# RWKV-7 recurrence on one core: centring, key transposes and variance on parts of the array, the solve written beside the inner product, and state updates and inverse steps pinned in program order

## The chip, the core and the metric

The kernel runs on one core of one Trainium2 chip. The metric is the device time of one execution in microseconds (us). Nothing is shared with other cores. Engines are called as in the profile: PE is the matmul engine (PEld its weight loads), DVE the vector engine, ACT the scalar engine, POOL the general engine, SP the engine that issues most DMAs.

## What is computed

Sixteen learned tokens and 256 tokens, 272 in all, with 2048 features go through two layers, each a token mixer and a squared-ReLU MLP. Layer 0 mixes by RWKV-7, layer 1 by gated linear attention (GLA). The change lies wholly in layer 0's recurrence, whose 32 heads of 64 features each carry a 64x64 state, and in what stands right behind it: a group norm for each head, a bonus, a gate and the output projection. Cut to that:

```python
def step(S, inp):
    r_t, w_t, k_t, v_t, a_t, b_t = inp
    sa = jnp.einsum('bhvk,bhk->bhv', S, a_t)
    S = S * w_t[:, :, None, :] + sa[..., None] * b_t[:, :, None, :] + v_t[..., None] * k_t[:, :, None, :]
    y = jnp.einsum('bhvk,bhk->bhv', S, r_t)
    return S, y
...
_, y = lax.scan(step, S0, xs)
...
mu = jnp.mean(y, axis=-1, keepdims=True)
var = jnp.mean(jnp.square(y - mu), axis=-1, keepdims=True)
y = ((y - mu) * lax.rsqrt(var + RW_GN_EPS)).reshape(B, T, D) * ln_w + ln_b
bonus = (jnp.sum(rh * kh * r_k, axis=-1, keepdims=True) * vh).reshape(B, T, D)
out = ((y + bonus).astype(x.dtype) * g) @ w_o
```

## The kernel before, in words

**Chunks and groups.** The scan is done in chunks of 64 tokens: four full ones and a last one of 16 tokens (`c` = 0 to 4). The 2048 features lie as 16 tiles of 128 partitions by 272 tokens (`hres` holds v and later y; `rr` the bonus), two heads to a tile. The recurrence runs for two groups of 16 heads (`g` = 0 and 1, 8 tiles each), one after the other. Within a chunk the tokens depend on each other through a triangular matrix for each head, which is inverted; then the chunk is a row of small products.

**A chunk's products on PE**, in fp32, each function a batch of 64x64 products over the 16 heads: `centre` (L671) takes the values of a chunk, token-major and with the head's mean removed, into `uv`; `keys` (L684) transposes the keys into `bkt`; `inner` (L694) applies the scores within the chunk to the values; `state` (L720, L722) applies the carried state `S`, on quadrants of the array in an order written out by hand; `solve` (L731) applies the inverse; `carry` (L740) and `learn` (L746) sum the new state in a PSUM bank, from which DVE writes `S` with the decay (`tt(sb, pS, ...)` on L747, shown as L300, the helper's line); `emit` (L755) makes y. ACT copies results from PSUM (uv on L677 and L734, bkt on L686, the scaled copy `rs` on L702).

**The inverses.** `invert` (L542) runs 30 elimination steps of two DVE operations each on `sysA` (shown as `upd<-sysA` and `sysA<-sysA,upd`, L300) for a batch of blocks of 32 tokens, four batches in all (two chunks or three of each group); the result goes out by DMA and comes back into the score tiles `AM` (`AM<-invd`, L565), and `merge` (L648, L658) joins blocks of 32 to blocks of 64. `scores` (L525) makes the masked scores of the next batches (masks on DVE, L528).

**Norm.** `norm(g)` covers four feature tiles of a group at a time: squares on ACT, the sum over a head on PE (`self.bones`, L773), the gate's product (L776), a logarithm and an exponential on ACT, and the products and sums on DVE (L781, L300, L784).

**Weights beside it.** The v projection and the output projection run in the same stretch, spread between the phases: `R(n)` issues n steps of three fp32r products (`mm3`, L163 to L165: hi x hi, hi x lo, lo x hi). Their weights come by DMA in pieces of 128x1024 (`raw`, three buffers) and are split into `hi` by ACT (L140) and `lo` by DVE (L141), two halves each. One piece lasts eight steps, and the SP queue holds weight loads and the loads of the inverses in one order.

**Order.** Within `manual_schedule(engines={PE})` the PE instructions stand in program order; DVE, ACT and SP instructions are put in order by a scheduler. What stands where on PE is set by numbers: `GAPS` gives the R steps of each chunk ahead of the solve and ahead of `learn`, `MARK` the count of R steps at which each `merge` begins, and `some(inv, n)` how many inverse steps are written at a place. PSUM tags and buffers: `pj` 2, `pm` 1, `pt` 2, `pry` 1, `pu` 2.

Of the kernel before, what the change touches and what calls it, by code (L numbers as in the profile page):

```python
# [46 lines left out]
GAPS = [(4, 2), (4, 2), (4, 2), (4, 3), (5, 5)]  # L47

MARK = [120, 170, 244, 302]
# [5 lines left out]
class Kern:  # L55
# [242 lines left out]
    def rwkv(self, done):  # L298
# [243 lines left out]
        def invert(b):  # L542
# [9 lines left out]
            for s in range(1, 31):  # L552
                k, m = 31 - s, s
                w = self.t(lp, [P, 256], "upd", 1)[:n, : k * m].rearrange("p (a b) -> p a b", a=m)
                tt(w, X[:n, s : s + 1, s + 1 :].to_broadcast([n, m, k]), X[:n, :m, s : s + 1].to_broadcast([n, m, k]))
                tt(X[:n, :m, s + 1 :], X[:n, :m, s + 1 :], w, ALU.add)
                yield
# [107 lines left out]

        def centre(g, c):
            full, n, nr = geom(c)[:3]
            pv = self.pm()
            for p in range(4):
                for e in range(2):  # L670
                    nc.tensor.matmul(pv[64 * e : 64 * e + nr, p * P : (p + 1) * P], hres[:, 8 * g + 4 * e + p, c * C : c * C + nr],  # L671
                                     self.cent, start=True, stop=True)
            x = uvs[g, c] = self.t(kp, [P, 16, 64], "uv", 2)
            if not full:
                nc.gpsimd.memset(x[0 : 2 * n], 0.0)
            for e in range(2):
                nc.scalar.copy(x[:nr, 8 * e : 8 * e + 8], pv[64 * e : 64 * e + nr].rearrange("p (h v) -> p h v", h=8))  # L677

        def keys(g, c):
            bkts[g, c] = self.t(kp, [P, 8, P], "bkt", 1)  # L680
            for e in range(2):
                pb = self.pm() if e else self.ptr()
                for p in range(4):
                    nc.tensor.transpose(pb[:, p * P : (p + 1) * P], BKs[c > 1][:, 4 * e + p, c % 2 * 128 : c % 2 * 128 + 128],  # L684
                                        self.ident)
                nc.scalar.copy(bkts[g, c][:, 4 * e : 4 * e + 4], pb.rearrange("p (h v) -> p h v", h=4))  # L686


        def inner(g, c):
# [3 lines left out]
            for h in range(16):  # L693
                nc.tensor.matmul(ra[at[h % 2], h // 2], am[:n, h, :n], uv[:n, h], start=h < 2, stop=c == 0 and h > 13)  # L694
            if c == 0:
# [29 lines left out]
        def solve(g, c):  # L725
            full, n, nr, am, lo, up, at = geom(c)
            uv, rs, pu = uvs[g, c], ras[g, c, "rs"], bank(self.pu())
            nu = n if full else 16
            for h in range(16):
# [592 lines left out]
```

## Time and profile before

| what | value |
|---|---|
| median of three runs | 2402.7 us (2400.86 to 2403.1) |
| the profiled execution | 2402.54 us |
| its span | 2400.8 us |
| granted PE clock, mean | 0.997 |
| PE busy | 2360.9 us |
| DVE busy | 1611.9 us |
| ACT busy | 1242.4 us |

Engine rows give busy time, share of the span and the number of instructions. A timeline row gives start, duration, engine, line, operation, output and inputs, tile and shape, and in brackets the idle time before it and what ended it. The records of matmuls overlap, so the cost of a matmul is read as the distance from one start to the next. In a fp32 product an instruction leaves two records.

### The profile page before, as it was taken

The page shows a single profiled execution, that of the slowest core. Times are in us where ns is not written, and L with a number is a line of the kernel's source. Part 1 is how long each engine was busy: PE and PEld are TensorE (multiplying, and loading weights), DVE is VectorE, ACT ScalarE, POOL GpSimd, SP SyncE. Part 2 cuts the span into 40 slices and gives each one's busy share as a digit, 9 for nine tenths or more (in the row PEclk, how much of TensorE's full clock was granted, in tenths as well). Part 3 has the DMA queues.
Part 4 walks back from the last instruction along what each step waited for, and adds up shares of the span by engine and source line. Part 5 has one row for each costly group of instructions (what it writes and reads, how often), then busy time and mean ns, then how long its engine had stood idle before and what let it go on. Part 6 is the DMA issues. An engine that isn't in the chain of part 4 may idle for free. (4 is left out here: it accounts for less than half of the span.)

```text
span 2400.8 us, 48047 instructions
## 1 busy us (share of the span) xinstructions
PE 2360.9 (98%) x19689; PEld 2244.1 (93%) x19689; DVE 1611.9 (67%) x2734; ACT 1242.4 (52%) x1975; POOL 6.6 (0%) x20
## 2 busy tenths in 40 slices
PE   9999999899999999999999999999999999999998
PEld 8888888889999999999999999999999999999997
DVE  8777886858655555555556777767666666666666
ACT  6376644556555445445345556555555445445444
POOL 0000000000000000000000000000000000000000
PEclk9999999999999999999999999999999999999999
DMA  6578864524555555555555554455555555555554
GB/s 210 169 235 293 248 190 146 146 83 163 183 187 193 187 191 191 188 193 186 192 189 190 196 181 167 159 176 193 182 201 200 200 201 200 202 202 202 201 201 169
DMA packets 160732, 455.34 MB, mean 190 GB/s; under 512 B 34112, under 2 KB 50624, under 8 KB 160512
## 3 DMA queue, kind: packets, MB, share of 16 engines
q1 hardware_dynamic: 160512, 452.27, 55.8%
q8 instruction: 154, 2.52, 0.4%
q14 instruction: 66, 0.54, 0.1%
HBM read 433.86 MB, written 18.35 MB: 188 GB/s over the span
## 5 line engine op out<-in xcount | busy, mean ns | idle before, releaser
L141 DVE TENSOR_TENSOR lo<-raw,hi 128x1024 fp32r<-128x1024 f32 (+1 forms) x818 | 927.4, 1140 | 534.1 <-ACT hi L140 525.9
L140 ACT CAST hi<-raw 128x1024 fp32r<-128x1024 f32 (+1 forms) x818 | 794.6, 979 | 939.4 <-PE pj L164 546.8
L163 PE MATMUL pj<-x,hi 128*128 128x272 f32 (+1 forms) x2624 | 748.6, 285 | 1.7 <-DVE hres L300 1.0
L165 PE MATMUL pj<-x,lo 128*128 128x272 f32 (+1 forms) x2624 | 734.5, 280 | 4.3 <-DVE lo L141 4.1
L164 PE MATMUL pj<-x,hi 128*128 128x272 f32 (+1 forms) x2624 | 734.0, 280 | 0.2 <-DVE x L240 0.2
L163 PEld LDWEIGHTS pj<-x,hi 128*128 128x128 f32 x2624 | 498.1, 190 | 10.2 <-issue 3.7
L165 PEld LDWEIGHTS pj<-x,lo 128*128 128x128 f32 x2624 | 498.2, 190 | 7.2 <-DVE lo L141 6.5
L164 PEld LDWEIGHTS pj<-x,hi 128*128 128x128 f32 x2624 | 498.2, 190 | 3.6 <-issue 1.4
L196 PE MATMUL pj<-x,hi 128*128 128x512 f32 x1280 | 419.9, 382 | 0.1
L197 PE MATMUL pj<-x,lo 128*128 128x256 f32 x1280 | 348.8, 273 | 0.0
L196 PE MATMUL pj<-h,hi 128*128 128x512 f32 x1008 | 330.3, 382 | 0.0
L163 PE MATMUL pj<-h,hi 128*128 128x272 f32 (+1 forms) x1040 | 290.1, 279 | 0.0
L164 PE MATMUL pj<-h,hi 128*128 128x272 f32 (+1 forms) x1040 | 290.1, 279 | 0.0
L165 PE MATMUL pj<-h,lo 128*128 128x272 f32 (+1 forms) x1040 | 290.1, 279 | 0.0
L197 PE MATMUL pj<-h,lo 128*128 128x256 f32 x1008 | 274.8, 273 | 0.0
L196 PEld LDWEIGHTS pj<-x,hi 128*128 128x128 f32 x1280 | 241.9, 189 | 34.1 <-DVE x L996 0.4
L197 PEld LDWEIGHTS pj<-x,lo 128*128 128x128 f32 x1280 | 245.7, 192 | 0.3 <-DVE lo L141 0.2
L196 PEld LDWEIGHTS pj<-h,hi 128*128 128x128 f32 x1008 | 190.5, 189 | 26.5
L163 PEld LDWEIGHTS pj<-h,hi 128*128 128x128 f32 x1040 | 196.6, 189 | 0.0
L164 PEld LDWEIGHTS pj<-h,hi 128*128 128x128 f32 x1040 | 196.6, 189 | 0.0
L165 PEld LDWEIGHTS pj<-h,lo 128*128 128x128 f32 x1040 | 196.6, 189 | 0.0
L197 PEld LDWEIGHTS pj<-h,lo 128*128 128x128 f32 x1008 | 193.5, 192 | 0.0
(270 smaller groups left out, 2077.2 us busy)
## 6 DMA issues: line engine op xcount, KB each, us to landing
raw<-mlp_w_d SPq DMA_DIRECT2D x512, 512.0 KB, 3.3
raw<-gla_in_d SPq DMA_DIRECT2D x98, 512.0 KB, 3.2
raw<-w_rkv_d SPq DMA_DIRECT2D x80, 512.0 KB, 3.9
raw<-gla_o_d SPq DMA_DIRECT2D x32, 512.0 KB, 4.3
raw<-w_r_d SPq DMA_DIRECT2D x16, 512.0 KB, 3.3
raw<-rw_oQ_d SPq DMA_DIRECT2D x16, 512.0 KB, 3.2
ard<-ar SPq DMA_DIRECT2D x16, 288.0 KB, 3.4
bkd<-bk SPq DMA_DIRECT2D x16, 288.0 KB, 3.5
```

The costliest lines, as they stand in the source:

```text
L140: nc.scalar.copy(hi[:, h], raw[:, h])
L141: nc.vector.tensor_tensor(out=lo[:, h], in0=raw[:, h], in1=hi[:, h].bitcast(F32), op=ALU.subtract)
L163: nc.tensor.matmul(out, hi[:, ws], xh, start=first, stop=False)
L164: nc.tensor.matmul(out, hi[:, ws], xl, start=False, stop=False)
L165: nc.tensor.matmul(out, lo[:, ws], xh, start=False, stop=last)
L196: nc.tensor.matmul(wide, hi[:, ws], xt, start=kt == 0, stop=False)
L197: nc.tensor.matmul(one, lo[:, ws], xt[:, 0], start=False, stop=kt == nk - 1)
```

## The change

Centring (`centre`) is done for two chunks at once, in four quadrants of 64x64 each, into two PSUM banks (`pm` and `pt`); `uv` gets three buffers, and centring is called for chunks 0 and 1, 2 and 3, and 4. `keys` makes 16 half-row transposes on 64 partitions each, in two banks. `solve(c)` and `inner(c + 1)` are issued alternately, head by head, for the first three chunks. In `norm`, the variance of two feature tiles is made together in four quadrants, two banks; the squares of all four tiles are made first (`ysq` four buffers), the gate weights are loaded two tiles ahead, and the logarithm of the second tile is done in two halves. The state update and the inverse steps of the batches behind the first are kept in program order on DVE. `GAPS`, `MARK` and the counts of inverse steps are new, and `scores(2, ...)` all lie in the merge of chunk 2.

On DVE, in group 0, the update of `S` behind chunk 0 stood behind step 10 of the inverse (`128x10x21`). Before:

```order
L300 TENSOR_TENSOR upd_4394<-sysA_1980 128x210
L300 TENSOR_TENSOR sysA_1980<-sysA_1980,upd_4394 128x10x21
L300 TENSOR_TENSOR S_3508<-pu_4428,WC_105 128x512
L300 TENSOR_TENSOR upd_4443<-sysA_1980 128x220
L300 TENSOR_TENSOR sysA_1980<-sysA_1980,upd_4443 128x11x20
```

And now, at the same place in the program:

```order
L300 TENSOR_TENSOR upd_4507<-sysA_1980 128x240
L300 TENSOR_TENSOR sysA_1980<-sysA_1980,upd_4507 128x16x15
L300 TENSOR_TENSOR upd_4510<-sysA_1980 128x238
L300 TENSOR_TENSOR sysA_1980<-sysA_1980,upd_4510 128x17x14
L300 TENSOR_TENSOR S_3508<-pu_4513,WC_105 128x512
L300 TENSOR_TENSOR upd_4571<-sysA_1980 128x234
```

The update has moved behind step 17 (`128x17x14`); which step it stands behind is now what the program writes.

On DVE in group 1, where `norm(1)` (rows `ysq`, `r` and `hres`) and the inverse run beside each other. Before, with step 5 of the inverse written around the first tile of the norm and step 6 behind it:

```order
L300 TENSOR_TENSOR sysA_1980<-sysA_1980,upd_6121 128x4x27
L300 TENSOR_TENSOR upd_6124<-sysA_1980 128x130
L781 SCALAR_TENSOR_TENSOR ysq_5885<-hres_72,vecs_126,ysq_5885 128x272
L300 TENSOR_TENSOR sysA_1980<-sysA_1980,upd_6124 128x5x26
L300 TENSOR_TENSOR r_19_93<-r_19_93,ysq_5885 128x272
L300 TENSOR_TENSOR upd_6163<-sysA_1980 128x150
L784 SCALAR_TENSOR_TENSOR hres_72<-r_19_93,vecs_126,pt_5997 128x272
```

Now (the lines of the norm are 810 and 813 in the new file; `ysq_5972` is the third tile of the norm):

```order
L300 TENSOR_TENSOR hres_72<-pj_6122,hres_72 128x272
L810 SCALAR_TENSOR_TENSOR ysq_5972<-hres_72,vecs_126,ysq_5972 128x272
L141 TENSOR_TENSOR lo_6275<-raw_6272,hi_6274 128x512 x2
L300 TENSOR_TENSOR r_21_95<-r_21_95,ysq_5972 128x272
L300 TENSOR_TENSOR upd_6256<-sysA_1980 128x84
L813 SCALAR_TENSOR_TENSOR hres_72<-r_21_95,vecs_126,pt_6230 128x272
L300 TENSOR_TENSOR sysA_1980<-sysA_1980,upd_6256 128x3x28
L810 SCALAR_TENSOR_TENSOR ysq_5974<-hres_72,vecs_126,ysq_5974 128x272
L300 TENSOR_TENSOR upd_6259<-sysA_1980 128x108
```

Step 3 (`128x3x28`) and all that follow have moved behind the third tile of the norm, and the update of `S` behind chunk 0 of group 1 stands behind step 16 there, where it stood behind step 14 before.

On PE, in group 0, the first solve (L731) was followed by the centring of chunk 1 (L671), and its inner product (L694) came behind `learn` (L746). Before:

```order
L731 MATMUL pu_4397<-rs_4352,AM_402_1979 64x64 x16
L671 MATMUL pm_4416<-cst_125,hres_72 64x128 x8
...
L746 MATMUL pu_4428<-uv_4298,bkt_4308 64x64 x16
L694 MATMUL pu_4484<-uv_4425,AM_402_1979 64x64 x16
L755 MATMUL pry_4501<-AM_402_1979,uv_4298 64x64 x16
```

Now solve (L742) and inner product (L702) alternate, and weight products follow:

```order
L742 MATMUL pu_4445<-rs_4415,AM_402_1979 64x64
L702 MATMUL pu_4447<-uv_4375,AM_402_1979 64x64
...
L742 MATMUL pu_4445<-rs_4415,AM_402_1979 64x64
L702 MATMUL pu_4447<-uv_4375,AM_402_1979 64x64
L163 MATMUL pj_4328<-x_1904,hi_4380 128x272
L164 MATMUL pj_4328<-x_1904,hi_4380 128x272
```

The inner product has moved ahead of `learn` and into the solve. The diff:

```diff
@@ -44,9 +44,9 @@
-GAPS = [(4, 2), (4, 2), (4, 2), (4, 3), (5, 5)]
-
-MARK = [120, 170, 244, 302]
+GAPS = [(2, 4), (5, 3), (5, 4), (4, 5), (5, 5)]
+
+MARK = [120, 180, 244, 308]
@@ -552,8 +552,9 @@
             for s in range(1, 31):
...
                 w = self.t(lp, [P, 256], "upd", 1)[:n, : k * m].rearrange("p (a b) -> p a b", a=m)
-                tt(w, X[:n, s : s + 1, s + 1 :].to_broadcast([n, m, k]), X[:n, :m, s : s + 1].to_broadcast([n, m, k]))
-                tt(X[:n, :m, s + 1 :], X[:n, :m, s + 1 :], w, ALU.add)
+                keep = tc.keep_in_program_order if b else lambda x: x
+                keep(tt(w, X[:n, s : s + 1, s + 1 :].to_broadcast([n, m, k]), X[:n, :m, s : s + 1].to_broadcast([n, m, k])))
+                keep(tt(X[:n, :m, s + 1 :], X[:n, :m, s + 1 :], w, ALU.add))
                 yield
             for rows in some_rows:
@@ -663,27 +664,34 @@
...
+        half = lambda q: slice(HEAD * q, HEAD * q + HEAD)
+        heads = lambda x: x.rearrange("p (h v) -> p h v", h=8)
+
         def centre(g, c):
             full, n, nr = geom(c)[:3]
-            pv = self.pm()
-            for p in range(4):
-                for e in range(2):
-                    nc.tensor.matmul(pv[64 * e : 64 * e + nr, p * P : (p + 1) * P], hres[:, 8 * g + 4 * e + p, c * C : c * C + nr],
-                                     self.cent, start=True, stop=True)
-            x = uvs[g, c] = self.t(kp, [P, 16, 64], "uv", 2)
-            if not full:
-                nc.gpsimd.memset(x[0 : 2 * n], 0.0)
-            for e in range(2):
-                nc.scalar.copy(x[:nr, 8 * e : 8 * e + 8], pv[64 * e : 64 * e + nr].rearrange("p (h v) -> p h v", h=8))
+            pvs = [self.pm(), self.ptr()]
+            for p in range(8):
+                for i in range(1 + full):
+                    for q in range(2):
+                        o = (c + i) * C
+                        nc.tensor.matmul(pvs[q][64 * i : 64 * i + nr, p * HEAD : (p + 1) * HEAD],
+                                         hres[half(q), 8 * g + p, o : o + nr], self.cent[half(q), half(q)], start=True, stop=True)
+            for i in range(1 + full):
+                x = uvs[g, c + i] = self.t(kp, [P, 16, 64], "uv", 3)
+                if not full:
+                    nc.gpsimd.memset(x[0 : 2 * n], 0.0)
+                for q in range(2):
+                    nc.scalar.copy(x[:nr, q::2], heads(pvs[q][64 * i : 64 * i + nr]))
         def keys(g, c):
-            bkts[g, c] = self.t(kp, [P, 8, P], "bkt", 1)
-            for e in range(2):
-                pb = self.pm() if e else self.ptr()
-                for p in range(4):
-                    nc.tensor.transpose(pb[:, p * P : (p + 1) * P], BKs[c > 1][:, 4 * e + p, c % 2 * 128 : c % 2 * 128 + 128],
-                                        self.ident)
-                nc.scalar.copy(bkts[g, c][:, 4 * e : 4 * e + 4], pb.rearrange("p (h v) -> p h v", h=4))
+            x = bkts[g, c] = self.t(kp, [P, 8, P], "bkt", 1)
+            pbs = [self.ptr(), self.pm()]
+            for f in range(8):
+                for q in range(2):
+                    nc.tensor.transpose(pbs[q][:, f * HEAD : (f + 1) * HEAD],
+                                        BKs[c > 1][half(q), f, c % 2 * 128 : c % 2 * 128 + 128], self.ident[half(q), half(q)])
+            for q in range(2):
+                nc.scalar.copy(x[:, :, half(q)], heads(pbs[q]))
         def inner(g, c):
@@ -692,6 +700,8 @@
...
             for h in range(16):
                 nc.tensor.matmul(ra[at[h % 2], h // 2], am[:n, h, :n], uv[:n, h], start=h < 2, stop=c == 0 and h > 13)
+                if h < 15:
+                    yield
             if c == 0:
@@ -722,13 +732,15 @@
...
-        def solve(g, c):
+        def solve(g, c, beside=False):
             full, n, nr, am, lo, up, at = geom(c)
...
             nu = n if full else 16
+            other = inner(g, c + 1) if beside else iter(())
             for h in range(16):
...
                 nc.tensor.matmul(pu[o : o + nu, h // 2], am[up, h, :nu], rs[up, h], start=True, stop=True)
+                next(other, None)
             for q in range(2):
@@ -744,7 +756,7 @@
             for h in range(16):
...
                 nc.tensor.matmul(pS[k, h // 2], bkts[g, c][:, h // 2, k], uv[:, h], start=c == 0 and h < 2, stop=h > 13)
-            tt(sb, pS, WC[:, 8 * g : 8 * g + 8, c : c + 1].to_broadcast([P, 8, HEAD]))
+            tc.keep_in_program_order(tt(sb, pS, WC[:, 8 * g : 8 * g + 8, c : c + 1].to_broadcast([P, 8, HEAD])))
         def emit(g, c):
@@ -757,27 +769,44 @@
...
         def norm(g):
+            fs = range(4 * g, 4 * g + 4)
+            sqs, g2s = {}, {}
             def square(f):
-                sq = self.t(kp, [P, T], "ysq", 2)
-                nc.scalar.activation(sq, hres[:, f], AF.Square)
-                return sq
-
-            nxt = square(4 * g)
+                if f in fs:
+                    sqs[f] = self.t(kp, [P, T], "ysq", 4)
+                    nc.scalar.activation(sqs[f], hres[:, f], AF.Square)
+
+            def load(f):
+                if f in fs:
+                    g2s[f] = self.t(kp, [P, 2, P], "g2", 2)
+                    nc.sync.dma_start(g2s[f], ap["g2"][f])
+
+            def spread(sq, va, x, y):
+                nc.scalar.activation(sq[x], va[y], AF.Ln, scale=1.0 / HEAD, bias=self.eps[GN_EPS][x])
+
+            for i in range(2):
+                load(fs[i])
+            for i in range(4):
+                square(fs[i])
             yield
-            for f in range(4 * g, 4 * g + 4):
-                sq = nxt
-                g2 = self.t(kp, [P, 2, P], "g2", 2)
-                nc.sync.dma_start(g2, ap["g2"][f])
-                va = self.pry()[:, :T]
-                nc.tensor.matmul(va, self.bones, sq, start=True, stop=True)
+            for f in fs:
+                if f % 2 == 0:
+                    vas = [self.pry()[:, :T], self.pm()[:, :T]]
+                    for i in range(2):
+                        for q in range(2):
+                            nc.tensor.matmul(vas[i][half(q ^ i)], self.bones[half(q), half(q)], sqs[f + i][half(q)],
+                                             start=True, stop=True)
                 pg = (self.ptr() if g else self.pu())[:, :T]
                 for i in range(2):
-                    nc.tensor.matmul(pg, g2[:, i], gs[i], start=i == 0, stop=i == 1)
-                nc.scalar.activation(sq, va, AF.Ln, scale=1.0 / HEAD, bias=self.eps[GN_EPS])
+                    nc.tensor.matmul(pg, g2s[f][:, i], gs[i], start=i == 0, stop=i == 1)
+                load(f + 2)
+                if f % 2 == 0:
+                    spread(sqs[f], vas[0], slice(0, P), slice(0, P))
+                    for q in range(2):
+                        spread(sqs[f + 1], vas[1], half(q), half(1 - q))
+                sq = sqs[f]
                 nc.scalar.activation(sq, sq, AF.Exp, scale=-0.5)
-                if f < 4 * g + 3:
-                    nxt = square(f + 1)
                 nc.vector.scalar_tensor_tensor(out=sq, in0=hres[:, f], scalar=self.vec("ln_w", f), in1=sq, op0=ALU.mult,
@@ -920,56 +949,57 @@
...
                 inv = invert(2 * g + 1)
-                some(inv, 3)
+                some(inv, 3 if g else 9)
                 until(128 + 128 * g)
+                keys(g, 0)
+                some(last, 1)
+                R(3)
                 centre(g, 0)
                 some(last, 1)
-                R(2)
-                keys(g, 0)
-                some(last, 1)
-                R(2)
-                inner(g, 0)
+                R(4)
+                some(inner(g, 0), 99)
                 for _ in last:
...
                 for c in range(5):
+                    steps = (5, 3, 5) if g else (5, 4, 6) if c < 2 else (0, 0, 6) if c == 2 else (4, 3, 6)
                     if c == 2:
...
                         some(inv, 99)
-                        if g == 0:
-                            scores(2, 0, 0)
                         until(MARK[2 * g + 1])
...
                         next(m)
+                        if g == 0:
+                            scores(2, 0, 0)
                         R(4)
                         next(m)
-                        R(4)
+                        if g == 0:
+                            for x in ((0, 1), (1, 0), (1, 1)):
+                                scores(2, *x)
+                                R(3)
+                            inv = invert(2)
+                        else:
+                            R(4)
                     if c:
                         state(g, c)
+                    if c in (1, 3):
+                        centre(g, c + 1)
                     if g == 0 and c == 1:
                         fetch(2, ARs, ard)
-                    if g == 0 and c == 2:
-                        scores(2, 0, 1)
                     R(GAPS[c][0])
-                    some(inv, 8)
-                    solve(g, c)
-                    if c < 4:
-                        centre(g, c + 1)
-                    if g == 0 and c == 2:
-                        scores(2, 1, 0)
+                    some(inv, steps[0])
+                    solve(g, c, c < 3)
+                    if c == 3:
+                        some(inner(g, 4), 99)
+                    R(GAPS[c][1])
+                    some(inv, steps[1])
                     if c < 4:
                         carry(g, c)
-                    R(GAPS[c][1])
-                    some(inv, 8)
-
-                    if c < 4:
                         learn(g, c)
-                        inner(g, c + 1)
-                    if g == 0 and c == 2:
-                        scores(2, 1, 1)
-                        inv = invert(2)
                     emit(g, c)
+                    if c == 3:
+                        R(2)
                     if c < 3:
@@ -979,7 +1009,7 @@
...
                             fetch(3, ARs, ard)
-                    some(inv, 5)
+                    some(inv, steps[2])
             for g in (2, 3):
                 for _ in norm(g):
```

## The prediction

> **What bounds the kernel now.** I read the engine shares on the page first, then two windows of the recurrence (roughly 330 to 565 us, the only stretch that the change touches), then the waits of the matmul engine (PE) in it, then its timeline.
>
> ```profile
> PE 2360.9 (98%) x19689; PEld 2244.1 (93%) x19689; DVE 1611.9 (67%) x2734; ACT 1242.4 (52%) x1975; POOL 6.6 (0%) x20
> ```
>
> Two windows of core 0 (us, then busy time of PE, PEld, DVE, ACT and POOL with instructions, granted clock, DMA share, GB/s):
>
> ```profile
> 380.00:400.00 20.00, 20.00 (x369) 17.90 (x370) 7.41 (x12) 9.92 (x19) 0.95 (x1) 0.91 0.30 79
> 420.00:447.00 27.00, 24.92 (x217) 21.78 (x215) 26.12 (x66) 10.77 (x24) 0.00 (x0) 1.00 0.46 126
> ```
>
> And PE's waits between 285 and 620 us (in all, times, longest):
>
> ```profile
> PE pt L658 <- DMA AM<-invd: 4.4, 2, 3.5
> PE pj L165 <- DVE lo L141: 2.1, 2, 1.0
> ```
>
> PE is busy 98% of the span, so the time is PE's issue time plus its waits. The second window shows that one stretch is different: while group 0 is normalised and the last score masks are made, DVE is busy 26.1 of 27 us and PE 24.9. The waits are short. One of them, in the timeline:
>
> ```profile
> 377.60 0.24 PE L658 MATMUL pt<-AM,rs 32*32 32x32 f32 x2
> 378.73 1.19 PE L658 MATMUL pt<-AM,rs 32*32 32x32 f32 x62 [0.89 <-DMA AM<-invd]
> ```
>
> The hole costs 1.1 us from start to start, and behind it the window 380 to 400 has a granted clock of 0.91: 0.09 x 20 = 1.8 us of clock lost. So a wait here is paid twice.
>
> The Trainium skill, TensorE: Matmul & The Clock Gate, Part 1: The HAM clock gate, says that the clock is halved after an idle window of about 3.4 us. By that rule a hole of 1.1 us would cost nothing more; the 0.91 speaks against it, and the sum goes by the row.
>
> **The change, part by part.** Prices first, as start-to-start times on PE:
>
> ```profile
> 329.79 0.28 PE L165 MATMUL pj<-x,lo 128*128 128x272 f32 x1
> ...
> 332.92 0.28 PE L165 MATMUL pj<-x,lo 128*128 128x272 f32 x1
> ...
> 336.98 0.38 PE L163 MATMUL pj<-x,hi 128*128 128x272 f32 x1
> ...
> 338.56 1.09 PE L671 MATMUL pm<-cst,hres 128*64 128x128 f32 x14
> 340.15 0.43 PE L671 MATMUL pm<-cst,hres 128*64 128x128 f32 x2 [0.50 <-ACT hres L816]
> 340.52 0.38 PE L163 MATMUL pj<-x,hi 128*128 128x272 f32 x1
> ...
> 346.29 0.28 PE L165 MATMUL pj<-x,lo 128*128 128x272 f32 x1
> 346.49 1.15 PE L731 MATMUL pu<-rs,AM 64*64 64x64 f32 x32
> 347.57 1.09 PE L671 MATMUL pm<-cst,hres 128*64 128x128 f32 x16
> 348.60 0.38 PE L163 MATMUL pj<-x,hi 128*128 128x272 f32 x1
> ```
>
> 27 weight products lie between 329.79 and 332.92: 0.116 each, so R(n) is 0.35n. From 346.29 to 346.49 is 0.20 instead of 0.116, and about as much is lost on the way back: leaving the weight products and returning costs 0.2. A solve is 1.08 and a centring 1.03.
>
> *Solving beside inner product.* A solve (L731) and an inner product (L694), 32 records each, are written alternately on opposite quadrants, 6 times (three chunks of two groups). If four quadrants run at once, a pair takes 1.08 instead of 2.16, and 6 x 1.08 = 6.5 us go. The nearest row is the state product, which already alternates:
>
> ```profile
> 352.73 0.66 PE L684 MATMUL pt<-cst,BK 128*128 128x128 f32 x4
> ...
> 353.75 0.27 PE L722 MATMUL pu<-S,AR 64*64 64x64 f32 x1
> ...
> 353.77 0.27 PE L722 MATMUL pu<-S,AR 64*64 64x64 f32 x1
> ...
> 355.24 0.38 PE L163 MATMUL pj<-x,hi 128*128 128x272 f32 x1
> ```
>
> Its 64 records take 353.75 to 355.24 = 1.49, and only its first part is interleaved. So a pair costs 1.08 to 1.49; I take 1.08, since all of its records alternate; the other end gives 2.5 us back.
>
> *Centring in quadrants.* Ten calls of 1.03 become four double ones (64 records, 1.08) and two single ones (32 records, taken as 1.05): 10.3 - 6.4 = 3.9 us. The other end of a double one is 1.49, as above.
>
> *Key transposes in halves.* Eight calls of 1.02 (352.73 to 353.75) become eight of 16 half-row transposes. The GLA layer has such products:
>
> ```profile
> 1367.39 0.40 PE L1133 MATMUL pt<-cst,vs 64*128 64x64 f32 x6
> 1367.72 0.38 PE L163 MATMUL pj<-x,hi 128*128 128x272 f32 x1
> ```
>
> Six take 0.33, so 16 take at most 0.88; a quarter of the old time per record (half the columns, two row halves side by side) gives 0.51. I take the middle, 0.70, and against a mean of 0.95 for the eight calls (not all of them start after a full drain) 2.0 us go; bounds 0.6 and 3.5.
>
> *Variance in quadrants.*
>
> ```profile
> 538.97 0.62 PE L773 MATMUL pry<-ysq,cst 128*128 128x272 f32 x2
> 539.43 1.08 PE L776 MATMUL pt<-gs,g 128*128 128x272 f32 x4
> ```
>
> One variance product is 0.46. Sixteen become eight pairs, four quadrants each: 3.7 us go; if a pair runs as two halves one behind the other, nothing goes. The pair writes two banks, each from two row halves at once.
>
> The Trainium skill, TensorEngine Tiling (Array Packing), Restrictions and Gotchas, warns that different row tiles can't reach one PSUM bank at the same time. By that the 3.7 would be nothing and the sum 3.7 higher. The two L722 records above are of different row halves, write one bank and start 0.02 apart with 0.27 each, which speaks against it.
>
> Three more returns to the weight products cost 0.6. **Work of PE: 6.5 + 3.9 + 2.0 + 3.7 - 0.6 = 15.5 us less.**
>
> *Waits that go.* The merge wait at 377.60 with its clock, 1.1 + 1.8 = 2.9: the merge comes ten R later in the new marks. The wait for the last column at 338.56 (1.96 instead of 1.03) and its like in group 1, since keys and three R stand ahead of the centring: 1.9. One late weight piece, 0.9 (the L165 row). Together 5.7. The longer merge wait (3.5) stays: its load is issued behind the same weight load.
>
> *The state update pinned behind the inverse.* This decides. On DVE in program order:
>
> ```profile
> 340.77 0.18 DVE L300 TENSOR_TENSOR upd<-sysA 128x30 f32<-128x30 f32 x1
> ...
> 341.72 0.25 DVE L300 TENSOR_TENSOR upd<-sysA 128x84 f32<-128x84 f32 x1
> ...
> 346.44 1.29 DVE L141 TENSOR_TENSOR lo<-raw,hi 128x512 fp32r<-128x512 f32 x2 [2.50 <-ACT hi L140]
> ...
> 351.01 0.68 DVE L300 TENSOR_TENSOR S<-pu,WC 128x512 f32<-128x512 f32 x1
> ...
> 356.84 0.41 DVE L300 TENSOR_TENSOR upd<-sysA 128x238 f32<-128x238 f32 x1
> ...
> 357.72 0.40 DVE L300 TENSOR_TENSOR upd<-sysA 128x234 f32<-128x234 f32 x1
> ```
>
> Before, S follows step 10; now steps 1 to 17 and one weight pair are ahead of it. From 340.77 to 357.72 are 17 steps with an idle of 2.5, a weight pair of 1.2 and S of 0.7: 12.5 us of steps. S would end at 340.77 + 12.5 + 1.2 + 0.7 = 355.2. PE leaves the merge at 336.98 and has 19 R (6.6), five returns (1.0) and 6.7 of phases to the state product, so it is there at 351.3. The wait is 3.9; with the half us that DVE may idle for the weight pair and the half that a hole costs beyond its idle (0.93 for 0.50 above), 4.8. I add 0.9 for the clock, half of the 1.8 above.
>
> Group 1 is worse. There steps 3 to 16 stand behind the third squared tile of norm(1), whose variance product now runs only after the inner product. On ACT:
>
> ```profile
> 344.39 1.21 ACT L702 ACTIVATE rs<-pu 64x512 f32<-64x512 f32 x2 [1.26 <-PE pu L694]
> ...
> 472.33 0.48 ACT L777 ACTIVATE ysq<-pry,eps 128x272 f32<-128x272 f32 x1
> ```
>
> On DVE:
>
> ```profile
> 471.23 0.50 DVE L781 SCALAR_TENSOR_TENSOR ysq<-hres,vecs,ysq 128x272 f32<-128x272 f32 x1
> 471.64 0.38 DVE L300 TENSOR_TENSOR upd<-sysA 128x220 f32<-128x220 f32 x1
> 471.94 0.44 DVE L300 TENSOR_TENSOR r<-r,ysq 128x272 f32<-128x272 f32 x1
> 472.29 0.44 DVE L300 TENSOR_TENSOR hres<-pj,hres 128x272 f32<-128x272 f32 x1
> 472.64 1.29 DVE L141 TENSOR_TENSOR lo<-raw,hi 128x512 fp32r<-128x512 f32 x2
> 473.84 0.49 DVE L784 SCALAR_TENSOR_TENSOR hres<-r,vecs,pt 128x272 f32<-128x272 f32 x1
> ```
>
> From the inner product's end ACT has the scaled copy rs (1.2), three logarithms (0.5 each) and an exponential: 3.5 with the product itself in part. Then DVE has two ysq (0.41), two r (0.35), two last products (0.41), two adds and three subtractions (0.35 each), two weight pairs (1.2) = 6.5, and steps 3 to 16: 12.5 less the first two (341.72 - 340.77 = 0.95) and the 17th (0.88), 10.7. S is written 3.5 + 17.2 + 0.7 = 21.4 after the inner product. PE has 16 R (5.6), the rest of norm(1) (1.9), three phases (3.2), keys 0.7 and returns 0.5 ahead: 11.9. Wait 9.5, and its clock 1.7. Behind S stand steps 17 onward and the next weight pair, with slack.
>
> *Smaller waits.* All four scores of batch 2 now lie in the merge of chunk 2, right behind its stages, in the same two PSUM banks:
>
> ```profile
> 372.28 1.29 DVE L300 TENSOR_TENSOR AM<-pt,cst 128x512 f32<-128x512 f32 x2
> ```
>
> A call needs both banks back, about 1.3 us by this mask pair, twice not covered by R: 2.6, bounds 0 and 5. In the stretch of the 420 to 447 window DVE is full, so what PE saves on variance there (1.8) comes back as waits for masks: 2.0. A variance pair behind keys needs its bank copied out: 1.5. The copies of uv ahead of carry 0.8, a later load for the last merge 1.0. **New waits: 4.8 + 0.9 + 9.5 + 1.7 + 2.6 + 2.0 + 1.5 + 0.8 + 1.0 = 24.8.**
>
> **Sum:** -15.5 - 5.7 + 24.8 = +3.6. The profiled execution took 2402.54 us (span 2400.8), the median of the runs is 2402.7, so nothing is to be corrected: 2406.
>
> **Rivals.** (a) *The state updates are not late.* If the group's S finds its data and DVE is there in time, 4.8 + 0.9 + 9.5 + 1.7 = 16.9 go: 2389. In between, if group 1's exponential or weight pairs come some us earlier than I stack them, 2394 to 2399. For it: DVE is busy only two thirds of the span, and my 21.4 puts every item in series. Against it: the program order, and the full DVE ahead of it. (b) *The quadrants don't run four at a time*, the change doing less than it says: solve and inner 1.49 (+2.5), double centring (+1.6), keys (+1.4), variance nothing saved (+3.7): 9 more, 2415, and slower on work alone by the same waits. It decides at a pair above about 1.3 us. (c) *The merges' loads miss one weight piece more.* The load of the inverse stands in SP's queue behind weight loads; one boundary (eight R, 2.8 us) later with a clock loss of 1.8 gives 2411.
>
> **How the numbers follow.** Forecast 0.44, rival (a) 0.36, (b) 0.12, (c) 0.08. The forecast's own range is 2400 to 2412 (bounds of the scores term and of keys). The whole range reaches from (a) entire to just above (b): 2388 to 2417. 0.2%, about what a measurement of this kernel tells from no change, is 4.8 us: faster is below 2397.7, slower above 2407.3. (a) gives 0.33 faster and 0.03 same; the forecast 0.03 faster, 0.25 same, 0.16 slower; (b) and (c) slower: 0.36, 0.28, 0.36.
>
> **What would show it.** Waits of the state product (L732 and L730 in the new file) for DVE S: two, about 4 and 9 us, none for (a). Sixty-four records of L742 and L702 within 1.1 us, or 1.5 for (b). A double centring at 1.1, keys at 0.7, the variance's four products at 0.5. No wait at 377 for the inverse's load; one of 3.5 in the third merge. The granted clock below 1 behind the S waits. The forecast is wrong if the S updates leave on time, or if DVE's order under load delays other things, masks above all, by more than my 2 to 3 us each.

## The result, and the profile after

The changed kernel takes **2416.5 us** (median of 5 runs, 2410.7 to 2418.3) against 2402.7 before (median of 5): ratio **1.0057, 95% interval 1.0047 to 1.0068**. It is slower by about 14 us. The profiled execution has a span of 2415.1 us.

The page's engine line, after:

```profile
PE 2358.1 (98%) x19945; PEld 2238.2 (93%) x19945; DVE 1613.5 (67%) x2734; ACT 1245.6 (52%) x1983; POOL 6.6 (0%) x20
```

PE is busy 2.8 us less. That is not the gain of the packing: busy time doesn't show waits, and an instruction that takes longer at a lower granted clock counts as more work in it. Windows of the recurrence, after (the columns as in the prediction):

```profile
380.00:400.00 20.00, 18.36 (x302) 16.35 (x302) 8.95 (x15) 6.54 (x15) 0.00 (x0) 0.83 0.29 80
420.00:447.00 27.00, 24.63 (x296) 20.09 (x293) 25.45 (x65) 13.50 (x30) 0.00 (x0) 1.00 0.51 155
480.00:520.00 40.00, 31.15 (x604) 28.24 (x604) 34.06 (x87) 16.75 (x32) 0.95 (x1) 0.91 0.35 102
```

The granted clock between 380 and 400 is lower than before (0.83 for 0.91), and there is a new stretch, 480 to 520, in which PE is busy 31 of 40 us and DVE 34. The stretch of norm(0), 420 to 447, is as full on DVE as it was (25.5 for 26.1 us). What PE waits for, after (285 to 640 us; in all, times, longest):

```profile
PE pu L732 <- DVE S L300: 6.8, 3, 3.4
PE pt L659 <- DMA AM<-invd: 5.1, 2, 2.9
PE pj L163 <- DVE hres L300: 5.0, 4, 4.0
PE pt L525 <- DVE AM L300: 2.4, 6, 0.5
PE pj L165 <- DVE lo L141: 2.1, 2, 1.1
...
PE pm L798 <- ACT bkt L694: 1.3, 1, 1.3
```

Three lines are new or grown: the state product waits for `S`, a weight product waits for an output sum (`hres`) that DVE has not yet taken from its bank, and both merges of group 1 wait for the inverse's load where only one did. Before, nothing waited for `S` in this stretch, and the wait for `hres` was short:

```profile
PE pj L163 <- DVE hres L300: 1.0, 3, 0.3
```

The places after, in PE's timeline:

```profile
357.36 0.37 PE L732 MATMUL pu<-S,AR 64*64 64x64 f32 x1 [3.39 <-DVE S L300]
...
457.12 1.19 PE L659 MATMUL pt<-AM,rs 32*32 32x32 f32 x62 [2.12 <-DMA AM<-invd]
...
482.54 0.35 PE L163 MATMUL pj<-x,hi 128*128 128x272 f32 x1 [3.96 <-DVE hres L300]
...
493.63 0.36 PE L732 MATMUL pu<-S,AR 64*64 64x64 f32 x1 [2.95 <-DVE S L300]
...
520.88 1.91 PE L659 MATMUL pt<-AM,rs 32*32 32x32 f32 x62 [2.95 <-DMA AM<-invd]
```

The packed products cost what follows, from start to start (rows of after: keys, then the first variance row of norm(1) behind them; a variance pair of norm(2), whose four rows are two banks; and the weight product behind its gate):

```profile
462.89 0.27 PE L691 MATMUL pt<-cst,BK 64*128 64x64 f32 x1
...
463.53 0.68 PE L798 MATMUL pry<-ysq,cst 64*64 64x272 f32 x4
...
557.57 0.45 PE L798 MATMUL pry<-ysq,cst 64*64 64x272 f32 x2
...
558.18 1.18 PE L802 MATMUL pt<-gs,g 128*128 128x272 f32 x4
559.00 0.48 PE L163 MATMUL pj<-x,hi 128*128 128x272 f32 x1
```

And the double centring of group 1, up to the gate behind it:

```profile
468.22 0.27 PE L677 MATMUL pm<-cst,hres 64*64 64x64 f32 x1
...
469.31 0.50 PE L802 MATMUL pt<-gs,g 128*128 128x272 f32 x1
```

Keys take 463.53 - 462.89 = 0.64 instead of 1.02; a variance pair takes 558.18 - 557.57 = 0.61 instead of 2 x 0.46, and the gate behind it 0.82 instead of 0.71. A double centring takes 1.09, and so does a solve with an inner product in chunk 2 of both groups (64 records). The pairs of the chunks before it take longer: 2.10 and 1.43 in group 0, 1.92 (at a granted clock of 0.50) and 1.43 in group 1.

For the comparisons below the recurrence is cut at the first stage of each of the four merges and at step 838, which is counted from the start of the program over all steps of three fp32r products and lies 88 R steps behind the fourth merge before and 82 after. Of each stretch the R steps are taken off at 0.347 us each: what is left is all other work and all waits. Before, the first stretch is 333.13 to 374.88 = 41.75 us with 50 R steps: 41.75 - 17.35 = 24.4. One execution each, in us:

| kernel | to 2nd merge | to 3rd | to 4th | to step 838 | sum |
|---|---|---|---|---|---|
| before | 24.4 | 46.5 | 35.3 | 35.2 | 141.3 |
| after | 24.9 | 49.9 | 40.7 | 39.1 | 154.6 |
| after, no pins | 24.9 | 53.7 | 28.8 | 33.1 | 140.5 |
| after, only S pinned | 25.9 | 54.0 | 29.2 | 33.1 | 142.1 |
| after, only inverse pinned | 24.9 | 50.0 | 44.3 | 37.3 | 156.5 |
| before with the packed phases | 22.9 | 46.3 | 34.5 | 33.3 | 137.1 |

The loss of 13.3 us lies in the last three stretches, and most of it, 9.3, behind the third merge. Differences of a few us are not to be read from this table: the first merge, ahead of which PE has the same program in all of these kernels, is reached anywhere between 330.4 and 335.0 us.

### The profile page after: what moved, and what is told of

Its sections match the earlier page's. It is cut to its first block, busy times and chain, and to the rows that moved or that the text cites. A ratio compares the mean times of both kernels' runs of the same rounds, so it can differ in the third digit from the quotient of the medians.

```text
span 2415.1 us, 48589 instructions
## 1 busy us (share of the span) xinstructions
PE 2358.1 (98%) x19945; PEld 2238.2 (93%) x19945; DVE 1613.5 (67%) x2734; ACT 1245.6 (52%) x1983; POOL 6.6 (0%) x20
## 5 line engine op out<-in xcount | busy, mean ns | idle before, releaser
L141 DVE TENSOR_TENSOR lo<-raw,hi 128x1024 fp32r<-128x1024 f32 (+1 forms) x818 | 927.6, 1141 | 542.0 <-ACT hi L140 533.8
```

What stands on the lines that cost most here:

```text
L141: nc.vector.tensor_tensor(out=lo[:, h], in0=raw[:, h], in1=hi[:, h].bitcast(F32), op=ALU.subtract)
```

## The experiments

Theory A: the pinned order on DVE makes the loss. Theory B: any shorter PE phase would have brought it, since the same DVE and ACT work then has less to hide behind. Ratios are to the kernel before, run on the same chip.

**1. No pins** (a_nopin).

```diff
-                keep = tc.keep_in_program_order if b else lambda x: x
+                keep = lambda x: x
...
-            tc.keep_in_program_order(tt(sb, pS, WC[:, 8 * g : 8 * g + 8, c : c + 1].to_broadcast([P, 8, HEAD])))
+            tt(sb, pS, WC[:, 8 * g : 8 * g + 8, c : c + 1].to_broadcast([P, 8, HEAD]))
```

> The changed kernel without any pin: state updates and inverse steps are again put in order by the scheduler. Theory A (the pinned DVE order makes the loss: the first state update behind step 17, and in group 1 the inverse held behind the third tile of the norm): the state update moves to behind step 13, four steps of 0.85 us earlier, and steps 3 onward move into the DVE idle time ahead of the third tile. The wait of 3.5 us for S in group 0 falls under 1, the 5.0 for a late output sum and the 3.0 for S in group 1 nearly go, the last merge's load wait of 3.9 shrinks: 2400 to 2406. Theory B (packing leaves PE too little time in which to hide the same DVE and ACT work, in whatever order): within 3 us of the changed kernel, 2413 to 2419.

Measured 2402.1 us, ratio 0.9998 (0.9988 to 1.0007). The 14 us are gone: theory A. No gain is left either: in the table the stretch to the third merge is 7.3 us longer than before, the next 6.5 shorter.

**2. The pins in the kernel before** (b_pin): the same two lines, the other way round, in the kernel before.

> The kernel before with only the two pins added, with its own counts of inverse steps. Theory A: in group 0 the state update stands behind step 17 and about two more (ends near 358.5 where PE asks at 353.75), in group 1 behind step 24 or so; waits of about 5 and 8 us with some clock loss: 2413 to 2420. Theory B: the pins themselves cost little, 2402 to 2406.

Measured 2435.9 us, ratio 1.0145 (1.0131 to 1.0158), more than expected. Its waits:

```profile
PE pu L723 <- DVE S L300: 29.3, 3, 13.4
PE pu L777 <- DMA g<-g_d: 4.2, 1, 4.2
```

With its own counts (8, 8 and 5 steps to a chunk) more steps are written ahead of S than in the changed kernel; pinned, they are all run ahead of it, and PE stands 29.3 us for S, and 4.2 for the load of a gate weight.

**3. Each pin alone**, by one or the other of the lines of experiment 1. Only the S pin taken away (a_nopinS):

> The changed kernel with the inverse steps pinned and the state updates free. The first S moves from step 17 to step 13 in group 0 and from step 16 to step 11 in group 1, while the inverse of group 1 still stands behind the third tile of the norm. If the place of S carries the loss: 2402 to 2406. If the held inverse does (late output sums, 5.0, and the last merge's load, 3.9 with clock): 2409 to 2413.

Measured 2414.6 us, ratio 1.0053 (1.0039 to 1.0067), above both ranges and the same as the changed kernel within the intervals: not the place of S. Only the inverse pin taken away (a_nopinI):

> The changed kernel with only the state updates pinned, the inverse steps free. Freeing S alone left 2414.6. If it is the inverse steps' pin that costs, this one is like the kernel without pins: 2400 to 2405. If the two pins cost only together: 2408 to 2416, and S (behind step 17 again) should show waits of 3 us or more.

Measured 2400.8 us, ratio 0.9997 (0.9988 to 1.0006). The two by two:

| | S free | S pinned |
|---|---|---|
| inverse free | 2402.1 | 2400.8 |
| inverse pinned | 2414.6 | 2416.5 |

The pin on the inverse steps is the whole loss. The two kernels' waits make it plainer. S free, inverse pinned:

```profile
PE pj L163 <- DVE hres L300: 5.0, 4, 4.0
PE pt L659 <- DMA AM<-invd: 5.0, 2, 2.5
PE pj L163 <- DVE r L300: 4.7, 2, 3.9
PE pj L165 <- DVE lo L141: 4.4, 3, 2.3
```

S pinned, inverse free:

```profile
PE pu L732 <- DVE S L300: 6.8, 3, 3.4
PE pj L163 <- DVE hres L300: 3.0, 4, 1.9
PE pj L165 <- DVE lo L141: 2.0, 2, 1.0
```

In the first hardly anything waits for S (0.3 us in all), and other results of DVE (output sums, bonus sums, weights) are late in its place. In the second S is as late as in the changed kernel, 6.8 us in all, and the kernel is 14 to 16 us faster (by the ratios and by the medians). What has gone there is the wait of both merges. For the third merge the inverse is simply earlier: it is written out (`invd`) at 433.34 instead of 441.25. That has a price, which the table shows: up to the third merge the two kernels with a pinned inverse take 49.9 and 50.0, the two with a free one 53.7 and 54.0, since there the free steps stand ahead of a later state update (with only S pinned, PE waits 2.57 us for it at 424.79, and the weight products behind run at half the granted clock). Behind the third merge the free one wins it back and more. For the fourth merge the DVE rows of the third step of group 1's inverse say why; the changed kernel:

```profile
468.68 0.43 DVE L300 TENSOR_TENSOR x<-hres,x 128x272 fp32r<-128x272 f32 x1
...
474.93 0.44 DVE L300 TENSOR_TENSOR hres<-pj,hres 128x272 f32<-128x272 f32 x1 [2.55 <-PE pj L165]
476.21 0.50 DVE L810 SCALAR_TENSOR_TENSOR ysq<-hres,vecs,ysq 128x272 f32<-128x272 f32 x1 [0.84 <-ACT ysq L809]
...
478.28 0.24 DVE L300 TENSOR_TENSOR upd<-sysA 128x84 f32<-128x84 f32 x1
...
506.50 1.95 DVE L562 STREAM_TRANSPOSE sysA<-sysA 32x256 f32<-32x256 f32 x4
```

Only S pinned:

```profile
467.71 0.25 DVE L300 TENSOR_TENSOR upd<-sysA 128x84 f32<-128x84 f32 x1
...
500.20 1.96 DVE L562 STREAM_TRANSPOSE sysA<-sysA 32x256 f32<-32x256 f32 x4
```

Counted from the third merge (452.0 and 457.9 on PE), step 3 starts at 26.2 with the pin and at 9.9 without, and the inverse is done (the transposes) at 54.5 and at 42.3. With the pin DVE has only four short instructions between the one at 468.68 and the one at 476.21, because the next step stands behind the norm's third tile, which waits for PE and ACT; from 476 on it is full, everything else queues behind the steps, and the first load for the fourth merge comes 12 us later. A pin on the inverse of the third merge alone, which might keep those 4 us without the loss behind it, was not run.

**4. Inverse steps written earlier, pins kept** (a_early): in group 1 nine steps behind the merge and none beside the norm.

```diff
-                some(inv, 3 if g else 9)
+                some(inv, 9)
...
                 for _ in last:
                     R(4)
-                    some(inv, 3)
```

> The changed kernel with the inverse steps of group 1 written earlier: 9 behind the merge instead of 3, none in the two places beside the norm, so that S still stands behind step 16. Theory A: steps 3 to 8 (about 4 us) run in the 6 us that DVE idles between 468 and 476 us; the waits for the late output sum (5.0) and for S (3.0) shrink by 4 us together and the last merge's load comes 4 us earlier, which takes 2 to 4 off its wait: 2408 to 2412. Theory B: DVE work is the same, so within 2 us of the changed kernel.

Measured 2412.6 us, ratio 1.0051 (1.0038 to 1.0064), just above what was expected: 4 us less than the changed kernel by the medians, 1.4 by the ratios, and the intervals overlap, so a gain is likely but not shown. Its waits:

```profile
PE pt L659 <- DMA AM<-invd: 5.0, 2, 2.8
PE pj L163 <- DVE hres L300: 2.5, 4, 1.4
```

Step 3 starts at 466.05 and the wait for the output sum halves, as expected. The wait for the merges' loads stays, which was not: counted from the third merge, the last load for the fourth is issued 2.9 us earlier, but PE comes there 2.9 us earlier too. The idle time before step 3 can be a part of the cause and is not all of it.

**5. Few pinned steps ahead of S, more behind** (a_fit):

```diff
-                    steps = (5, 3, 5) if g else (5, 4, 6) if c < 2 else (0, 0, 6) if c == 2 else (4, 3, 6)
+                    steps = (0, 0, 10) if c < 2 else (0, 0, 6) if c == 2 else (2, 2, 9)
```

with a_early's edit.

> The changed kernel with both pins kept, but other counts of inverse steps: in both groups 8 steps stand ahead of the first state update and 10 behind it, ahead of the second. Theory A1 (the pins as such cost nothing; what costs is the number of pinned steps ahead of S, about 0.85 us each): S in group 0 is 9 steps earlier and on time, in group 1 8 steps earlier; no wait over 1 us for the first S, but the second S (behind step 18) may wait 2 to 4; 2398 to 2406. Theory A2 (any pin costs, since it keeps DVE from filling its idle time): 2410 to 2418. If the inverses end later the merge loads wait more, some 2 to 4 us on top.

Measured 2415.4 us, ratio 1.0060 (1.0047 to 1.0074): the range of A2. PE no longer waits for S at all, and waits for the inverses instead:

```profile
PE pt L649 <- DVE sysA L562: 10.1, 2, 5.9
PE pt L659 <- DMA AM<-invd: 5.9, 1, 5.9
```

On DVE, the two state updates of group 0:

```profile
350.08 0.69 DVE L300 TENSOR_TENSOR S<-pu,WC 128x512 f32<-128x512 f32 x1 [3.47 <-PE pu L758]
...
362.52 0.69 DVE L300 TENSOR_TENSOR S<-pu,WC 128x512 f32<-128x512 f32 x1 [1.84 <-PE pu L758]
```

Here DVE idles 3.5 and 1.8 us for `learn`, with inverse steps ready behind S that the pins hold back. Written ahead of S the steps make PE wait, written behind it they make DVE wait, and the inverse ends late: a loss of the same size either way. These are two ways to divide the steps; that one between them costs less is not excluded.

**6. The scores back in their places** (a_scores): the calls of scores(2, ...) ahead of the merge and behind state, solve and learn of chunk 2, as before.

> The changed kernel with the four scores of batch 2 put back to their places of before (one ahead of the merge, the others behind state, solve and learn of chunk 2). Theory C (their crowding in the merge costs 5.8 us against 2.7 in the kernel before, measured as extra time of the merge, scores and R segments there): 3 us less, 2412 to 2415. If the crowding is only where a delay from elsewhere shows, nothing changes: 2415 to 2418.

Measured 2413.8 us, ratio 1.0054 (1.0041 to 1.0067); 2.7 us below the changed kernel, but the intervals overlap. Its waits:

```profile
PE pu L732 <- DVE S L300: 12.9, 3, 7.1
...
PE pt L659 <- DMA AM<-invd: 1.8, 1, 1.8
```

The wait for S grew by 6.1 as that for the loads fell by 3.3: moved more than removed. Without pins, the same edit (a_nopin_sc):

> The changed kernel without pins and with the scores of batch 2 back in their old places. If the crowding costs as much as it did with pins (2.7 us) the two gains add: 2398 to 2400. If it only moved a wait: 2401 to 2404.

Measured 2401.4 us, ratio 1.0001 (0.9993 to 1.0010), against 2402.1: no difference. Without pins the crowding of the scores costs nothing that the measurement tells.

**7. The packed phases alone** (b_work): the new centring, keys and solve beside inner product with the new `GAPS`; norm, scores, `MARK` and step counts of before; no pins. Against the changed kernel, beside the pins' lines and the scores' calls:

```diff
-MARK = [120, 180, 244, 308]
+MARK = [120, 170, 244, 302]
...
-                some(inv, 3 if g else 9)
+                some(inv, 3)
...
-                    steps = (5, 3, 5) if g else (5, 4, 6) if c < 2 else (0, 0, 6) if c == 2 else (4, 3, 6)
+                    steps = (8, 8, 5)
```

and norm as before.

> The new centring, keys and solve beside inner product alone, with the norm, the places of scores, the marks and the step counts of before, and without pins (the R steps of each chunk as in the changed kernel, 2 ahead of the solve and 4 behind and so on). PE work falls by 6.4 for the pairs, 3.9 for centring, 2.5 for keys, about 13 in all. Theory A: part of it stays, S behind step 13 and the earlier norm give waits of 4 to 8: 2393 to 2399. Theory B (DVE and ACT set the pace of this stretch, whatever PE saves): 2400 to 2405.

Measured **2396.0 us, ratio 0.9973 (0.9964 to 0.9983)**: faster than both. Some 13 us of PE work go by the sum of the expectation, and 6 of them arrive. What waits now:

```profile
PE pj L163 <- DVE hres L300: 3.1, 4, 2.1
PE pt L659 <- DMA AM<-invd: 2.9, 1, 2.9
PE pj L163 <- DVE r L300: 2.9, 2, 1.5
PE pj L165 <- DVE lo L141: 2.7, 3, 1.0
PE pu L732 <- DVE S L300: 2.5, 2, 2.3
```

Two to three us at each of DVE's results, and one wait for a load: that much of theory B holds. All of PE's waits for DVE in this stretch add up to 6.0 us before and to 13.7 here, and the 7.7 more are about what is missing of the 13. With the shorter phases DVE is late by a little at each of its results.

**8. The other parts on top of it.** The new norm (b_work_norm):

> The version with the new centring, keys and solve beside inner product, plus the new norm (variance of two tiles in quadrants, squares all ahead). If the packed variance brings its work (8 pairs of 0.62 instead of 16 of 0.46 is 2.4, less 0.1 on each gate behind it): 2394 to 2396. If pairing it delays the norm's tiles and adds waits for banks (1.6 us for a bank behind keys in the changed kernel, the third tile behind the inner product): 2397 to 2401.

Measured 2396.1 us, ratio 0.9976 (0.9968 to 0.9985): the same as without. Its trace, of the longest of its twelve executions (2403.3), has a wait that experiment 7 has not, a variance pair that waits for the bank of the keys:

```profile
PE pm L798 <- ACT bkt L694: 1.3, 1, 1.3
```

The new marks and counts with the old norm (b_work_tab):

> The same version with the marks and step counts of the changed kernel, without pins, and with the old norm. The kernel without pins and with the scores back measured 2401.4 with the new norm; if the norm makes the difference to 2396, this is 2395 to 2398; if marks and counts do, 2399 to 2403.

Measured 2402.4 us, ratio 1.0002 (0.9993 to 1.0010): the marks and counts cost 6 us without any pin. So the parts add up: the packed phases bring 6 us, the norm (and, without pins, the places of the scores) nothing that the measurement tells, the marks and counts take the 6 us back, and the pin on the inverse costs the 14. Its waits for the inverse's load are of two merges, where experiment 7 has one:

```profile
PE pt L659 <- DMA AM<-invd: 5.9, 2, 3.9
```

**9. One merge moved** (b_best): experiment 7 with the second stage of the third merge behind keys and centring.

```diff
-                next(m)
+                if g == 0:
+                    next(m)
...
+                if g:
+                    next(m)
+                    R(3)
                 some(inner(g, 0), 99)
```

> The version with the new centring, keys and solve beside inner product, and the second stage of group 1's first merge moved behind keys and centring, 15 R steps behind the first stage instead of 4. In every kernel so far this stage waits for the inverse's load (3.1 us there) and half a clock follows it (1.9). If the wait is only one for the load, both go and about 1 us of waits for banks comes: 2391 to 2394. If the load stands behind one weight piece more by then, the wait comes back: 2395 to 2398.

Measured 2407.1 us, ratio 1.0023 (1.0014 to 1.0031): 11 us worse than experiment 7, against what was expected. (The expectation has a wait at this merge in every kernel; in the two whose inverse steps are free and whose scores lie in the merge, experiments 1 and 3, there is none.) The wait at the third merge did go (that stretch is 43.2 us for 46.3, counted as in the table). But at the fourth, on PE:

```profile
499.69 0.24 PE L659 MATMUL pt<-AM,rs 32*32 32x32 f32 x2
505.69 1.91 PE L659 MATMUL pt<-AM,rs 32*32 32x32 f32 x62 [5.75 <-DMA AM<-invd]
```

and in SP's queue:

```profile
493.94 0.35 SPq L132 DMA_DIRECT2D raw<-rw_oA_d  x1
494.34 0.42 SPq L566 DMA_DIRECT2D AM<-invd  x1
501.27 0.35 SPq L132 DMA_DIRECT2D raw<-rw_oA_d  x1
501.67 0.96 SPq L566 DMA_DIRECT2D AM<-invd  x2
```

The last loads of the inverse stand behind a weight load that was issued only at 501.27, right ahead of them and 1.3 us after PE had stopped. SP's queue stood 6.4 us at it, for DVE to have read the buffer (`lo`, L141, from 499.95 to 501.24). That came behind ACT's `hi` of 499.30, and this one right behind the merge's own copies on ACT (L652, from 497.77). What held `hi` back before those copies isn't shown. The stretch behind that merge is 8.4 us longer than in experiment 7 (41.7 for 33.3). In the stretch ahead of it PE also stands 5.1 us for an output sum (2.1 in experiment 7).

## Why the prediction was right or wrong

The time lies in the range given, at its upper edge, and that is luck: it is outside the forecast's own 2400 to 2412, and the range reached so far up only for rival (b), whose mechanism the trace shows to be absent but for a part in the variance. The forecast of 2406, within 0.2% of the time before, was 10.5 us too low, and slower by 0.57% is clear of the noise.

- **Work of PE, 15.5 us less:** right as work. The pairs (1.09 where nothing holds them up) and the double centrings (1.09) as forecast, keys 0.64 for 0.70. The variance pair is 0.61 instead of 0.46 and the gate behind it 0.1 longer, so that term was 1.7 and not 3.7; keys give 0.5 more, and `learn` (0.98) and `emit` (1.03) are a little shorter than their 1.08, which together gives most of it back. Rival (b) is out for the pairs, the centring and the keys, and in part true for the variance.
- **Waits that go, 5.7:** the waits did go, but others came in their place. Nothing waits at the second merge for a load, but the granted clock between 380 and 400 is 0.83 for 0.91, behind the waits of the crowded scores (counted there); the centring waits 0.6 for the bank of the keys now. The third merge's wait, which was to stay at 3.5, is 2.1. The variance pair behind keys waits 1.3, forecast 1.5.
- **S behind step 17 in group 0, 4.8 and 0.9 for the clock:** near in size. PE idles 3.39 us, and the state product behind it takes 2.27 instead of 1.49: 4.2 for the 5.7.
- **S behind step 16 in group 1, 9.5 and 1.7:** near in sum, in two places: 2.95 at S and, unforeseen, 3.96 at an output sum that DVE took late. The granted clock of 0.83 between 480 and 500 makes 3.4 more, 10.3 for the 11.2. The first pair of solve and inner product, 1.92 at half the clock, is in it.
- **"This decides":** wrong. The step that failed is that the pinned S was held to be what costs. Free S with pinned inverse steps gives nothing back that the measurement tells (2414.6), pinned S with free steps gives everything (2400.8). The inverse under its pin is late at whatever is next: S, an output sum, a weight, or a load for a merge.
- **The last merge's load, 1.0:** mis-sized, and the largest error of the sum. The merge's second stage took 5.03 us instead of 1.13, and the R steps and the state product behind it lost 1.4 and 0.7 at a low granted clock (0.55 from 520 to 525, 0.76 from 525 to 530): 6.0 in all. That is rival (c), weighed at 0.08, on top of the forecast rather than instead of it: between the first and the last of the four loads three weight loads stand in SP's queue, where there were two. What set it off is the inverse, which ends 54.5 us behind the third merge with the pin and 42.3 without.
- **The scores in the merge, 2.6:** 5.8 in the trace (merge stages 0.4 and 0.8, scores 3.5, R steps 1.1), above the bound of 5.
- **Not in the sum:** in group 0 the first pair of solve and inner product is held up for the scaled copy `rs` on ACT, 1.0.

The last three exceed the forecast by 5.0 + 3.2 + 1.0 = 9.2 us, most of the 10.5; the smaller misses above go both ways, and the rest is not booked term by term.

Rival (a) was wrong as put: S on time (experiment 5) is not faster.

## What to carry to other kernels

Where an engine in the middle (here DVE) serves several due times, a pin on its long batch can make every other result late or the engine idle, as here; look where the batch ends against the point that needs it, not only at the first thing that stands behind it. Bring in work savings without the new order first: the packed phases alone gave 0.27%, new marks and counts took it back, and the pin took 0.6%. A wait for a load that stands behind weight loads in one queue can move to the next such place when the time between them changes, as it did in experiment 9.

## What the runs showed of the hardware

Four quadrant products of 272 columns into two banks, each bank from two row halves, took 0.61 us, between one full product (0.46) and two (0.92); keys and centring, whose banks each take one row half, came out at 0.64 and 1.09. In the trace the first records of all four products start within 0.02 us (at 557.57, after). The Trainium skill, TensorEngine Tiling (Array Packing), Restrictions and Gotchas, rules out that two row tiles reach one bank at the same time; if they took turns throughout, the pair would take the 0.92, so the trace agrees at most in part. No run tells whether the shared bank is the reason.

The prediction lets a clock loss follow a wait as short as 0.89 us. That is not so at every wait: behind the 1.25 us for the bank of the keys (the variance pair at 465.46, after) the window of 463 to 475 us has a granted clock of 1.00, while behind the 3.39 us for S the state product runs at half the clock, 0.50.
